# Seven products for the gate half of a projection, values split at the PSUM eviction, and four decay gates moved into the heads

## The chip, the cores and the metric

The kernel runs on one core of one Trainium2 chip. The metric is the device time of one execution in microseconds (us). The core has five engines, each with its own instruction queue in order: TensorE (PE in the profile, with PEld for its weight loads), VectorE (DVE), ScalarE (ACT), GpSimd (POOL) and SyncE (SP, which here only issues DMAs). DMAs are issued from the queues of SP, ACT and POOL.

## The reference, cut to what matters

A trunk of two layers on 512 tokens of width 1024 in float32: a gated linear attention (GLA) with 4 heads, a gated FFN, a softmax attention, a second FFN. The change lies in the GLA alone:

```python
h = rmsnorm(x, norm_mix[0])
q, k, v, g, r = split(h @ w_in)            # 512, 512, 1024, 1024, 32 columns
la = log_sigmoid(r_dir @ w_up + b_up)/16   # for each direction and head: the decay "gates"
o  = gla_chunked(q, k, v, la_f) + flip(gla_chunked(flip(q), flip(k), flip(v), flip(la_b)))
x  = x + (rmsnorm(o, norm_w) * silu(g)) @ w_out
```

In `gla_chunked`, q and k are multiplied by exp of plus and minus the sums of la within chunks of 64 tokens; masked products within a chunk and a carried state across chunks give o.

## The kernel before, in words

**Number format.** Each float32 operand of a matmul is split into a high part (rounded to fp32r) and a low part (the rest), and a product is three matmuls: high by high, high by low, low by high. For weights, `Weights` (L145 on) does this: a piece of 128x1024 is loaded by SP into one of 5 `raw` buffers (L161), ScalarE copies the high part into one of 4 `wh` buffers, and VectorE subtracts for the low part into one of 4 `wl` buffers (`split`, L240). For the sources in `by_dma`, `low_dma` (L204) does without VectorE: ScalarE writes the high part and the negative of it, and a DMA from POOL's queue, issued by `flush` (L233), adds the original onto the negative. `piece` (L253) hands a piece to the matmuls and makes `ahead` more. For FFN weights marked as sums, `summed` (L209) forms differences of quarters, so that eight block products become seven.

**The GLA** (`gla`, L487) runs in this order:

1. The vg projection, x @ [v | g], token by token rows: four segments of 512 columns (v first half, v second half, g first half, g second half). A segment (`seg`, L498) is 8 slices of x's width (k) x 4 token blocks (j) x 3 matmuls of 128x128 by 128x512 (L440), into four PSUM banks; `seg_out` (L505) has VectorE scale each bank by the token's norm and write it in float32 to `v` or `g`.
2. After segment 0: the squares of x and the token norm (`ms`, L394; `rtok`, L398), the small projection r (`rp`, L541) and its split `rst`.
3. The gates: eight (4 heads x 2 directions). `gate(n)` (L555) is one matmul (z, L559), then Abs, Exp, Ln on ScalarE, a sum, a scan and small steps on VectorE, and three Exp. `GATE_STEPS` (L30) puts all eight beside the matmuls of segments 1 to 3 (`beside`, L593).
4. The heads, from L767: the k and q projections from `w_kq` (`kproj`, `qproj`, feature by feature, L408 to L410 through `feature_steps`), `factors` and `keys` (exp factors times q and k on VectorE, `end` on POOL), `rows` (transposes of the keys and their split, L652 to L655), `inner` (L668), `masked` (L675 to L681), `values` (L684: the head's columns of v are split, 16 pairs of a ScalarE copy at L690 and a VectorE subtraction at L691 in all), `outer` (the state, L711, and the chunk's own part, L724), `outputs` (L735), `gated` (norm and silu(g), L738), `tail` (transposes, L759). The order across heads is written out by hand in the loop at L773. Silu of g (L770) comes before head 0.
5. The out projection (`out_steps`, L450) with `x += ...` at L473.

**Order.** The program is a list of instructions without engines' queues; at build time a scheduler puts each engine's instructions in order by their place in the list and by estimates of when they are ready. `issue_after` forces one behind another. On the chip each queue is then fixed. Buffers with one tag turn over: `g` has 22 of 128x1024, `x` four of 128x1024 (x itself), `u` three, `t` five and `sq` three of 128x512; PSUM has `acc` 3, `s` 2, `pt` 2 and `po` 1 banks.

Of the kernel before, what the change touches and what calls it, by code (L numbers as in the profile page):

```python
# [29 lines left out]
GATE_STEPS, GATE_LAG = (1, 3, 5, 7, 10, 12, 15, 17), 2  # L30
# [42 lines left out]
def hybrid_encoder_kernel(  # L73
# [71 lines left out]
    class Weights:  # L145
# [3 lines left out]
        def __init__(self):  # L149
            self.todo, self.made, self.by_dma, self.pending = [], {}, [], []  # L150
            self.sums, self.last, self.fine = set(), None, []
            self.loaded, self.strip = {}, {}
            self.loads, self.wide, self.turn = LOADS, 0, 0

        def add(self, src, strips=None, pieces=2):
            for i in strips or range(src.shape[0]):
                self.todo += [(src, i, h) for h in range(pieces)]
                if pieces > 2:
                    self.sums.add((id(src), i))

# [11 lines left out]
        def load(self, key):  # L172
            src, i, h = key
            if (id(src), i) in self.sums:
# [7 lines left out]
        def make(self, key):  # L182
            src, i, h = key
            self.load(key)
# [104 lines left out]
    for a in (w_vg, w_kq, w_gout):  # L289
        W.add(a)  # L290
# [5 lines left out]
    W.by_dma += [(a, 1) for a in qk_order + [w_av]] + [(w_aout, 2)]  # L296
# [190 lines left out]
    def gla(norm, nxt):  # L487
# [7 lines left out]
        v = [big(F32, "v") for _ in range(NT)]  # L495
        g = [big(F32, "g") for _ in range(NT)]
# [16 lines left out]
        for c in range(KC):  # L513
            norm.square(c)
        norm.tokens()
        seg_out(ps, v, 0)
        sync.dma_start(mfull, scan_mask)
        smask = cp.tile([P, P], U8, name="smask")
        tri = gc[:, 896 : 896 + P]
        make_lower_triangular(nc, tri, val=1.0, diag=False)  # L520
        dve.tensor_copy(smask, tri)
        cw = cp.tile([P, 2 * 2 * FC * 4], F32, name="cw")


# [12 lines left out]
        pool.tensor_tensor(gst[64:96, :], graw[64:96, :], gst[64:96, :].bitcast(F32), ALU.subtract)  # L537
        rp = bank("acc", "rp")
# [7 lines left out]
        rst = sp.tile([P, S], F32R, tag="t", bufs=5, name="rst")  # L546
# [5 lines left out]
        EK, FK = {}, {}  # L552
        act.preload_act_table_set("natural_log_exp_and_others")

        def gate(n):  # L555
# [5 lines left out]
            a = tmp("u", "ga")  # L561
            act.activation(a, z, AF.Abs, bias=b)
            m = tmp("t", "gm")
# [24 lines left out]
            act.activation(fk[:, here], fk[:, here], AF.Exp, scale=1.0 / 16)  # L588
# [8 lines left out]

        seg_out(seg(1, beside), v, 1)
        seg_out(seg(2, lambda n: beside(KC + n)), g, 0)
        seg_out(seg(3, lambda n: beside(2 * KC + n)), g, 1)  # L600

        oh = [None] * KC

        def kproj(h):
            kqt = big(F32, "kq")
            psk = bank("acc" if h else "pt", "k")
            for last in feature_steps(*W.half(w_kq, 2 * h), norm.hl, psk):
# [8 lines left out]
        def qproj(h, kqt):  # L616
            psq = bank("acc" if h else "pt", "q")
            last = feature_tile(*W.half(w_kq, 2 * h + 1), norm.hl, psq)
# [65 lines left out]
        def values(h):  # L684

            th, tl = pair("wh", NH, F32R, "vrh"), pair("wl", NL, F32R, "vrl")
            for s in range(NT):
                r = v[s][:, h * DV : (h + 1) * DV]
                hi = th[:, s * DV : (s + 1) * DV]
                act.activation(hi, r, AF.Copy)  # L690
                dve.tensor_tensor(tl[:, s * DV : (s + 1) * DV], r, hi.bitcast(F32), ALU.subtract)  # L691
            return [(th[:, s * DV : (s + 1) * DV], tl[:, s * DV : (s + 1) * DV]) for s in range(NT)]
# [76 lines left out]
        for j in range(NT):  # L769
            on_act = act.activation(g[j], g[j], AF.Silu)  # L770
        last = qproj(0, kqt)

        for h in range(GH):  # L773
            factors(h, kqt)
            if h == 0:
# [8 lines left out]
            elif h < GH - 1:  # L784
                last = outputs(h - 1, st, og, last)
                gated(h - 1, og)
                kts, last = rows(h, ends, last)
                banks, last = inner(h, last)
                at = masked(banks)
                _, kqt = whole(kproj(h + 1))  # L790
# [607 lines left out]
```

## Time and profile before

| | |
|---|---|
| median of 3 runs | 1097.81 us (1097.74 to 1098.18) |
| the profiled execution, its own time | 1096.11 us |
| its span, first to last instruction | 1094.0 us |
| granted TensorE clock | 1.0 of full speed |
| vg projection, L440 with the gates' z beside it | 6.0 to 100.5 us |
| GLA heads | 100.5 to 178.6 us |
| out projection of the GLA to the next norm | 178.6 to 232.5 us |

One execution is profiled. Its page gives the busy time of each engine, the chain of work that ended last, and groups of instructions: line, engine, operation, tile names (out<-in), shapes and count, then busy us and the mean ns of one, then the idle time of the engine before them and who ended it. A matmul's own length overlaps its neighbours', so the time that a matmul takes is read from a row of many in the chain, not from the mean of its group. In lists of waits the numbers are the total in us, the times, and the longest.

### The profile page before, as it was taken

How to read it: one execution, taken by the hardware profiler on the slowest of the kernel's cores; microseconds unless marked ns; L12 is line 12 of the kernel's file. 1: busy time of each engine (PE TensorE's matmuls, PEld its weight loads, DVE VectorE, ACT ScalarE, POOL GpSimd, SP SyncE). 2: the span in 40 equal slices, each digit the busy share in tenths (PEclk: the TensorE clock that was granted, in tenths of full speed). 3: DMA queues.
4: the chain of work that ended last, by engine and by line, in shares of the span. 5: the costliest groups of instructions: out<-in, count | busy, mean ns of one | idle time of the engine just before them, and what ended most of it. 6: DMA issues, size and time to landing. Idle time of an engine off the chain costs nothing.

```text
span 1094.0 us, 17377 instructions
## 1 busy us (share of the span) xinstructions
PE 1086.3 (99%) x6716; PEld 975.8 (89%) x6716; DVE 870.8 (80%) x1301; ACT 683.1 (62%) x1086; POOL 126.6 (12%) x138
## 2 busy tenths in 40 slices
PE   9999999999999999999999999999999999999998
PEld 7888888888899999999988888788889999999997
DVE  6686776549999899988855578765999889998892
ACT  6565344459775676657664677746977567665660
POOL 0100123022000100010014343002100010001000
PEclk9999999999999999999999999999999999999999
DMA  7323123478634733365757474557944373226542
GB/s 274 133 96 96 58 78 110 139 186 204 152 99 115 155 117 97 95 157 134 248 137 165 122 222 144 169 173 186 216 106 135 98 161 114 101 88 154 135 174 77
DMA packets 52882, 153.76 MB, mean 141 GB/s; under 512 B 6208, under 2 KB 6720, under 8 KB 52800
## 3 DMA queue, kind: packets, MB, share of 16 engines
q1 hardware_dynamic: 36192, 110.56, 31.6%
q0 software_dynamic: 11712, 33.56, 16.9%
q10 hardware_dynamic: 4896, 8.55, 2.1%
q8 instruction: 52, 0.85, 0.3%
q14 instruction: 30, 0.25, 0.1%
HBM read 110.70 MB, written 14.68 MB: 115 GB/s over the span
## 4 chain that ended last, share of the span: by engine, by line
PE 96%; DVE 2%; ACT 1%; DMA 1%; issue 0%; SPq 0%; DVEq 0%; ACTq 0%
PE r L879 37%; PE vg L440 8%; PE op L466 8%; PE up L408 6%; PE up L409 6%; PE up L410 6%; PE dn L409 2%; PE dn L410 2%; PE dn L408 2%; PE av L440 1%; PE o L735 1%; PE A L408 1%; PE A L409 1%; PE A L410 1%; PE B L410 1%; PE B L408 1%
## 5 line engine op out<-in xcount | busy, mean ns | idle before, releaser
L248 DVE TENSOR_TENSOR wl<-raw,wh 128x1024 fp32r<-128x1024 f32 x152 | 185.2, 1220 | 34.1 <-ACT wh L247 33.9
L247 ACT ACTIVATE wh<-raw 128x1024 fp32r<-128x1024 f32 x152 | 158.5, 1052 | 84.4 <-PE op L466 22.6
L879 PE MATMUL r<-gu,wh 128*128 128x256 f32 x896 | 161.8, 283 | 0.0
L879 PE MATMUL r<-xt,wh 128*128 128x256 f32 x832 | 151.2, 283 | 0.0
L879 PEld LDWEIGHTS r<-gu,wh 128*128 128x128 f32 x896 | 140.2, 192 | 0.7
L879 PEld LDWEIGHTS r<-xt,wh 128*128 128x128 f32 x832 | 130.1, 192 | 0.5 <-ACT wh L247 0.2
L879 PE MATMUL r<-gu,wl 128*128 128x256 f32 x448 | 126.6, 283 | 0.0
L879 PE MATMUL r<-xt,wl 128*128 128x256 f32 x416 | 117.4, 283 | 0.0
L879 PE MATMUL r<-nh,wh 128*128 128x256 f32 x312 | 88.9, 285 | 0.7 <-ACT r L907 0.7
L879 PE MATMUL r<-nh,wl 128*128 128x256 f32 x312 | 88.3, 283 | 0.0
L879 PE MATMUL r<-nl,wh 128*128 128x256 f32 x312 | 88.3, 283 | 0.0
L879 PEld LDWEIGHTS r<-gu,wl 128*128 128x128 f32 x448 | 85.9, 192 | 0.0
L440 PE MATMUL vg<-wh,xhl 128*128 128x512 f32 x256 | 79.9, 390 | 1.0 <-DVE wh L245 1.0
L879 PEld LDWEIGHTS r<-xt,wl 128*128 128x128 f32 x416 | 79.7, 192 | 0.0
L409 PE MATMUL up<-nl,wh 128*128 128x512 f32 x192 | 74.9, 390 | 0.0
L408 PE MATMUL up<-nh,wh 128*128 128x512 f32 x192 | 74.9, 390 | 0.0
L410 PE MATMUL up<-nh,wl 128*128 128x512 f32 x192 | 74.7, 389 | 0.0
L466 PE MATMUL op<-oT,wh 128*128 128x512 f32 x256 | 72.1, 394 | 0.0
L879 PEld LDWEIGHTS r<-nh,wh 128*128 128x128 f32 x312 | 59.8, 192 | 3.1 <-ACT r L907 2.9
L879 PEld LDWEIGHTS r<-nl,wh 128*128 128x128 f32 x312 | 59.8, 192 | 0.2
L879 PEld LDWEIGHTS r<-nh,wl 128*128 128x128 f32 x312 | 59.8, 192 | 0.0
L440 PEld LDWEIGHTS vg<-wh,xhl 128*128 128x128 f32 x256 | 47.9, 188 | 11.4 <-ACT sq L382 1.2
(263 smaller groups left out, 2676.8 us busy)
## 6 DMA issues: line engine op xcount, KB each, us to landing
raw<-in_w_up_dram SPq DMA_DIRECT2D x84, 512.0 KB, 4.5
raw<-in_w_down_dram SPq DMA_DIRECT2D x44, 512.0 KB, 3.7
wl<-raw POOLq DMA_DIRECT2D x16, 512.0 KB, 5.2
ring<-p ACTq DMA_DIRECT2D x32, 256.0 KB, 2.7
raw<-in_w_vg_dram SPq DMA_DIRECT2D x12, 512.0 KB, 4.3
wl<-in_w_up_dram POOLq DMA_DIRECT2D x12, 512.0 KB, 7.9
raw<-in_w_kq_dram SPq DMA_DIRECT2D x8, 512.0 KB, 3.6
raw<-in_w_gout_dram SPq DMA_DIRECT2D x8, 512.0 KB, 3.7
```

The costliest lines, as they stand in the source:

```text
L247: act.activation(hi[:, sl], r[:, sl], AF.Copy)
L248: dve.tensor_tensor(lo[:, sl], r[:, sl], hi[:, sl].bitcast(F32), ALU.subtract)
L408: mm(ps, wh, mh, start=start, stop=False)
L409: mm(ps, wh, ml, start=False, stop=False)
L410: return mm(ps, wl, mh, start=False, stop=stop)
L440: mm(ps[j][:, :width], hl[k][i == 2][:, j * P : (j + 1) * P], (wl if i == 1 else wh)[:, sl], start=k == 0 and i == 0, stop=k == KC - 1 and ...
L466: mm(pss[ng][n], wt[:, sl], mv, start=k == 0 and i == 0, stop=k == KC - 1 and i == 2)
L735: last = mm(og[s], l, r, start=False, stop=i == len(parts) - 1, skip_group_check=True)
L879: mm(dst, w[:, sl], m, start=start and j == 0 and a == 0, stop=j == len(pairs) - 1 and a == 2, skip_group_check=True)
```

## The change

1. **Segments 2 and 3 (g) become seven block products** (`seg_seven`). Tokens are halved (near, far), the k slices are taken in pairs (even, odd), the 1024 columns are halved. The eight block products of this 2x2 by 2x2 scheme become seven, after Strassen and Winograd, each of 4 pairs x 2 token blocks x 3 matmuls of 512 columns, in the order 1, 7, 6, 4, 5, 2, 3, accumulating in three sets of two banks that are read between products: ScalarE for 1, 7 and 6, VectorE for 4, 5, 2 (adding onto g) and 3.
2. **Their operands**: `token_sums(p)` forms the four combinations of x's quarters for pair p: ScalarE scales x[2p] and x[2p+1] by the norm weights (2 of 128x512), VectorE adds and subtracts (4 of 128x256), and `low_dma` splits the result (2 of 128x1024 on ScalarE, a 512 KB accumulating DMA). Pairs 0 and 1 stand right behind segment 0's matmuls and ahead of the r weights, the squares and the norm; pairs 2 and 3 in segment 1. `make_vg` forms the weight combinations: a VectorE subtraction of 128x1024 for product 7, two for 6, one for 3, in each of two halves, besides the split of each of the 14 half products. Pieces are made 3 ahead.
3. **v leaves PSUM as high and low parts**: ScalarE writes the high part, VectorE subtracts. The low parts take the four `x` buffers, so x is loaded again from `xT` (eight DMAs on SP) after the last head's matmuls. `values` only takes slices.
4. **Gates**: 0 and 1 in segment 1, 2 and 3 in the sixth product, 4 and 5 in head 0 (at its start and behind its `outer`), 6 and 7 in head 1. The table for Exp and Ln is loaded again after Silu.
5. **All of w_kq by `low_dma`**, pieces 2 ahead; the first k and q projections use `s` banks; `rst` sits in an `sq` buffer.

The diff, cut to its core (branches that these constants never take, the renamed arguments and the new layout of w_vg on the host are left out; the layout stores the four quarters of g's weights in place of strips 4 to 7):

```diff
-GATE_STEPS, GATE_LAG = (1, 3, 5, 7, 10, 12, 15, 17), 2
+KQ_DMA = 4
+KQ_AHEAD = 2
+LATE_GATES = {0: (4,), 30: (5,), 1: (6,), 31: (7,)}
+SEVEN_BANKS = (("pt", "pt"), ("acc", "acc"), ("acc", "s"))
+GATE_STEPS, GATE_LAG = (1, 4, 18, 19, 99, 99, 99, 99), 1
+VG_ORDER = (1, 7, 6, 4, 5, 2, 3)
+VG_AHEAD = 3
+VG_RAW = {1: (4, "g"), 7: (5, "raw"), 6: (6, "raw"), 2: (7, "raw")}
+SUMS_FIRST = 2
+SUMS_AT = {0: 2, 2: 3}
...
+        def load_vg(self, i, half):
+            if i not in VG_RAW or (i, half) in self.vg:
+                return
+            strip, tag = VG_RAW[i]
+            self.vg[i, half] = t = big(F32, "raw") if tag == "g" else pair("raw", NR, F32, "raw")
+            sync.dma_start(t, w_vg[strip, :, half * 2 * S : (half + 1) * 2 * S])
+
+        def make_vg(self, i, half):
+            self.load_vg(i, half)
+            a11, a21, a22, a12 = (self.vg.get((n, half)) for n in (1, 7, 6, 2))
+            r = {1: a11, 6: a11, 4: a22, 5: a21, 2: a12, 3: a12}.get(i)
+            if i == 7:
+                r = pair("raw", NR, F32, "sum")
+                dve.tensor_tensor(r, a21, a11, ALU.subtract)
+            elif i == 6:
+                dve.tensor_tensor(a21, a21, a22, ALU.subtract)
+                dve.tensor_tensor(a11, a11, a21, ALU.subtract)
+            elif i == 3:
+                dve.tensor_tensor(a12, a12, a11, ALU.subtract)
+            hi, lo = self.two()
...
+                self.split(hi, lo, r)
+            return hi, lo
...
-    for a in (w_vg, w_kq, w_gout):
+    W.add(w_vg, range(4))
+    W.todo += [(w_vg, -i, half) for i in VG_ORDER for half in range(2)]
+    for a in (w_kq, w_gout):
         W.add(a)
...
-    W.by_dma += [(a, 1) for a in qk_order + [w_av]] + [(w_aout, 2)]
+    W.by_dma += [(w_kq, KQ_DMA)] + [(a, 1) for a in qk_order + [w_av]] + [(w_aout, 2)]
...
-        def seg_out(ps, dst, h):
+        def seg_out(ps, h):
             for j in range(NT):
-                o = dst[j][:, h * S : (h + 1) * S]
+                if h == 0:
+                    v[j] = v[j][0], pair("x", KC // 2, F32R, "vl")
+                hi, lo = (a[:, h * S : (h + 1) * S] for a in v[j])
                 r = norm.rtok[:, j : j + 1]
-                dve.tensor_scalar(o, ps[j], r, None, ALU.mult)
+                act.activation(hi, ps[j], AF.Copy, scale=r)
+                dve.scalar_tensor_tensor(lo, ps[j], r, hi.bitcast(F32), ALU.mult, ALU.subtract)
+
+        def token_sums(p):
+            y = big(F32, "xs")
+            for i in range(2):
+                act.activation(y[:, i * S : (i + 1) * S], x[2 * p + i], AF.Copy, scale=norm.weight(2 * p + i))
+            b11, b12, b21, b22 = (y[:, n * H : (n + 1) * H] for n in range(4))
+            dve.tensor_tensor(b11, b12, b11, ALU.subtract)
+            dve.tensor_tensor(b12, b12, b22, ALU.add)
+            dve.tensor_tensor(b22, b22, b11, ALU.add)
+            dve.tensor_tensor(b21, b21, b22, ALU.subtract)
+            hi, lo = big(F32R, "xt"), big(F32R, "xt")
+            W.low_dma(hi, lo, y)
...
+        def seg_seven(between):
+            r = lambda j: norm.rtok[:, j : j + 1]
+            near, far = slice(0, S), slice(S, 2 * S)
+            first, second, third = ([bank(tag, "vg") for tag in tags] for tags in SEVEN_BANKS)
+            n = 0
+            for i, ps in zip(VG_ORDER, (first, second, first, second, first, third, first)):
+                for half in range(2):
+                    wh, wl = W.piece(w_vg, -i, half, VG_AHEAD)
+                    for o in range(2):
+                        p, sl = 2 * half + o, slice(o * S, (o + 1) * S)
+                        xh, xl = q[p][i]
+                        for j in range(2):
+                            js = slice(j * P, (j + 1) * P)
+                            for a, (m, w) in enumerate(((xh, wh), (xh, wl), (xl, wh))):
+                                mm(ps[j], m[:, js], w[:, sl], start=i in (1, 7, 2) and p == 0 and a == 0,
+                                   stop=i in (4, 2, 3) and p == 3 and a == 2, skip_group_check=True)
+                        if o == 0:
+                            W.flush()
+                    between(n)
+                    n += 1
...
         ps = seg(0)
+        for p in range(SUMS_FIRST):
+            token_sums(p)
...
-        rst = sp.tile([P, S], F32R, tag="t", bufs=5, name="rst")
+        rst = sp.tile([P, S], F32R, tag="sq", bufs=3, name="rst")
...
-        seg_out(seg(1, beside), v, 1)
-        seg_out(seg(2, lambda n: beside(KC + n)), g, 0)
-        seg_out(seg(3, lambda n: beside(2 * KC + n)), g, 1)
+        seg_out(seg(1, beside_seg), 1)
+        g = [big(F32, "g") for _ in range(NT)]
+        seg_seven(lambda n: beside(KC + n))
...
         def values(h):
...
+            return [tuple(a[:, h * DV : (h + 1) * DV] for a in v[s]) for s in range(NT)]
...
+        with tc.issue_after(turns[max(turns)].ins):
+            for j in range(NT):
+                on_act = act.activation(g[j], g[j], AF.Silu)
+        with tc.issue_after(on_act.ins):
+            turns["table"] = act.preload_act_table_set("natural_log_exp_and_others")
...
         for h in range(GH):
+            gates_for(h)
             factors(h, kqt)
...
             st, og, last, on_dve = outer(h, kts, at, vs, last)
+            gates_for(h + 30)
...
+        for p, t in enumerate(x_tiles()):
+            for i in range(2):
+                sync.dma_start(x[2 * p + i], xT[(2 * p + i) * P : (2 * p + i + 1) * P, :])
```

More of the change, by code (lines that the diff above doesn't have):

```diff
@@ L605, in kproj @@
             kqt = big(F32, "kq")
-            psk = bank("acc" if h else "pt", "k")
-            for last in feature_steps(*W.half(w_kq, 2 * h), norm.hl, psk):
+            psk = bank("acc" if h else "s", "k")
+            for last in feature_steps(*W.half(w_kq, 2 * h, KQ_AHEAD), norm.hl, psk):
+                if h == 0:
+                    beside(next(late_gates))
                 yield last, kqt
@@ L616, in qproj @@
         def qproj(h, kqt):
-            psq = bank("acc" if h else "pt", "q")
-            last = feature_tile(*W.half(w_kq, 2 * h + 1), norm.hl, psq)
+            psq = bank("acc" if h else "s", "q")
+            last = feature_tile(*W.half(w_kq, 2 * h + 1, KQ_AHEAD), norm.hl, psq)
             dve.scalar_tensor_tensor(kqt[:, :S], psq, DK ** -0.5, norm.R, ALU.mult, ALU.mult)
```

108 lines of the change are left out of this document (75 added, 33 removed).

## The prediction

> **What bounds the kernel now.** I read the busy totals first, then who TensorE waited for, then the chain that ended last, then busy time by stage.
>
> ```profile
> span 1094.0 us, 17377 instructions
> PE 1086.3 (99%) x6716; PEld 975.8 (89%) x6716; DVE 870.8 (80%) x1301; ACT 683.1 (62%) x1086; POOL 126.6 (12%) x138
> ```
> ```profile
> PE warm L324 <- DVE bd L330: 1.3, 1, 1.3
> PE vg L440 <- DVE wh L245: 1.0, 1, 1.0
> PE r L879 <- ACT r L907: 0.7, 1, 0.7
> PE o L724 <- DVE atl L681: 0.3, 2, 0.2
> ```
> ```profile
> 29.09 3.79 PE rp L541 x16
> 84.18 16.32 PE vg L440 x72
> 176.93 1.64 PE o L724 x12
> ```
>
> TensorE (PE) is busy for 1086.3 of 1094.0 us, and its waits, listed as total, times and longest, are tenths of a microsecond after the start; inside the gated-linear-attention heads only the 0.3 us at L724 is named. So the kernel lasts as long as TensorE's list of matmuls, and a change pays by shortening the list, as long as no new wait opens. The third view gives the price of one 512-column matmul in the vg projection: 72 in 16.32 us, 0.2267 us each, one behind the other. (The 389 ns that the groups show for one is its length with the overlap.)
>
> Busy time by stage, each pair of numbers being busy us and instructions:
>
> ```profile
> 6.00:28.30 22.30, 22.30 (x99) 18.09 (x99) 17.61 (x28) 14.69 (x24) 0.00 (x0) 1.00 0.83 296
> 28.30:33.30 5.00, 5.00 (x30) 4.27 (x29) 2.98 (x7) 2.38 (x3) 3.77 (x4) 1.00 0.52 183
> 33.30:56.05 22.75, 22.75 (x102) 18.80 (x101) 16.23 (x25) 12.49 (x21) 0.12 (x1) 1.00 0.34 116
> 56.05:100.50 44.45, 44.45 (x197) 36.79 (x197) 34.42 (x53) 27.14 (x44) 0.00 (x0) 1.00 0.32 107
> 100.50:122.10 21.60, 21.43 (x117) 18.37 (x116) 13.97 (x21) 9.75 (x16) 2.08 (x2) 1.00 0.17 49
> 290.00:340.00 50.00, 50.00 (x355) 47.04 (x355) 47.80 (x69) 33.14 (x51) 0.00 (x0) 1.00 0.31 96
> ```
>
> The columns are PE, weight loads, DVE (VectorE), ACT (ScalarE), POOL, granted clock, DMA. The rows are segment 0 of vg, its end, segment 1, segments 2 and 3, the first part of the heads, and a piece of the first FFN. The last one matters: there VectorE is 47.80 of 50 us busy, 95.6%, beside the same kind of work (weights added, split, and read by seven products), and TensorE loses nothing.
>
> **The change part by part. (1) The matmuls.** Segments 2 and 3 are 2 x 8 x 4 x 3 = 192 matmuls of 512 columns. The seven products are 7 x 4 pairs of rows x 2 token blocks x 3 = 168 of the same shape, each with its own 128x128 stationary operand as before. 24 fewer at 0.2267 us: **-5.44 us**. All else on TensorE stays; four of the eight gate matmuls only move into the heads. The Trainium skill ("TensorE: Matmul & The Clock Gate", section "Back-to-back issue gap") gives a sustained 131 ns for a matmul of 512 columns in a real stream; by it 24 matmuls would be worth 3.1 us. The chain above disagrees with 226.7 ns, so I go by the chain.
>
> **(2) VectorE in the projection.** Prices:
>
> ```profile
> L248 DVE TENSOR_TENSOR wl<-raw,wh 128x1024 fp32r<-128x1024 f32 x152 | 185.2, 1220 | 34.1 <-ACT wh L247 33.9
> L247 ACT ACTIVATE wh<-raw 128x1024 fp32r<-128x1024 f32 x152 | 158.5, 1052 | 84.4 <-PE op L466 22.6 <-DVE raw L228 15.3 <-PE q L409 11.1
> L227 DVE TENSOR_TENSOR sum<-raw,raw 128x1024 f32<-128x1024 f32 x42 | 51.1, 1217 | 0.0
> L583 DVE TENSOR_TENSOR ga<-ga,t 128x256 f32<-128x256 f32 x6 | 2.5, 417 | 0.0
> L564 DVE TENSOR_SCALAR gm<-z,prm 128x512 f32<-128x512 f32 x5 | 3.7, 748 | 3.3 <-ACT ga L562 3.3
> L567 DVE TENSOR_TENSOR gm<-gm,ga 128x512 f32<-128x512 f32 x5 | 3.5, 691 | 1.3 <-ACT ga L566 1.2
> L572 DVE TENSOR_TENSOR_SCAN ga<-gconst,gm 128x512 f32<-128x512 f32 x3 | 3.7, 1221 | 0.1
> L580 DVE COPY t<-ga 128x4 f32<-128x4 f32 x6 | 1.0, 168 | 0.2
> L582 DVE TENSOR_TENSOR fk<-ga,t 128x3 f32<-128x3 f32 x6 | 1.0, 159 | 0.2
> ```
>
> A gate costs VectorE 0.748 + 0.691 + 1.221 + 0.168 + 0.159 + 0.417 = 3.40 us. From 28.3 to 100.5 us VectorE was busy 2.98 + 16.23 + 34.42 = 53.6 us. Out go four gates (-13.6) and the two kq splits that fell here (-2.4; their low parts now come by DMA). In come six more splits (14 pieces for 8: +7.3), eight subtractions of weights (product 7 one, 6 two, 3 one, in two halves each: +9.8) and the token sums of pairs 2 and 3 (8 x 0.417 = +3.3). The sixteen evictions stay sixteen, of about the same length. Sum 58.0 us, or 61.3 if pairs 0 and 1 spill over from segment 0. The stretch gets shorter: 72.2 - 5.44 - four gate matmuls (0.9) = 65.9 us. So VectorE is to be **88 to 93%** busy, below the 95.6% that cost nothing. Pieces are made three ahead, with four slots: piece n+3 may be split when piece n starts and is needed 3 x 12 x 0.2267 = 8.2 us later; its longest chain (two subtractions, ScalarE's copy of about 1.05 us, the low part) is 4.7 us. I cost this at 0. If the cover goes, the price is rival B's.
>
> **(3) The start.** The sums of pairs 0 and 1 are written ahead of the squares, which the token norm waits for.
>
> ```profile
> 19.48 1.36 ACT L382 ACTIVATE sq<-x 128x512 f32<-128x512 f32 x2 [0.76 <-DVE sq L386]
> 28.14 0.95 PE L394 MATMUL ms<-ones,sq 128*128 128x1 f32 x8
> L373 ACT ACTIVATE xhl<-x,prm 128x512 fp32r<-128x512 f32 x32 | 22.8, 712 | 9.0 <-DVE x L1030 2.7 <-DMA x<-in_xT_dram 2.1 <-DVE x L473 1.9
> ```
>
> ScalarE gets 4 x 0.712 + 4 x 1.05 = 7.0 us more, and segment 0 leaves it 22.30 - 14.69 = 7.6 us. So it fits, barely. The last square ended at 20.8 us; behind all of the added work, and behind the copies of rw and gst (1.9 us, estimated from L247 by their 768 and 1024 columns), it ends at 29.7 and its sum at 30.4, against 28.1 when the norm's matmuls start. Ends: 0 and 2.3 us. Some of the squares will fill gaps while the sums wait for VectorE, so I take the nearer third, **+0.8**. The v evictions become ScalarE's high part and then VectorE's low part: about 0.7 us later for a bank that segment 1 reads at its third token block, 0.7 us after 33.3 against 32.1: nothing.
>
> **(4) Low parts of kq by DMA.**
>
> ```profile
> wl<-raw POOLq DMA_DIRECT2D x16, 512.0 KB, 5.2
> DMA to landing us min/median/max: 3.6/6.2/9.1
> ```
>
> The first piece gets its slot when the twelfth of the fourteen half products starts; its low part is read 8.2 + 0.45 us later. Two copies (2.1) and a median landing of 5.2 make 7.3; with the longest landing of all accumulating DMAs, 9.1, it is 11.2. Ends 0 and 2.6; ScalarE also has a gate there, so **+0.3**. Later pieces are two ahead at 5.4 us each: 10.9 us of cover, 0. What waits behind a late low part is all of TensorE, in order. POOL's queue takes an issue of 0.9 us each time; ahead of the keys' products that is slack, since the keys are transposed only after the next projection.
>
> **(5) The heads.**
>
> ```profile
> L691 DVE TENSOR_TENSOR vrl<-v,vrh 128x256 fp32r<-128x256 f32 x16 | 9.1, 612 | 0.0
> L690 ACT ACTIVATE vrh<-v 128x256 fp32r<-128x256 f32 x16 | 5.4, 405 | 6.2 <-PE o L724 3.7 <-PE k L409 2.5
> L565 ACT ACTIVATE ga<-ga 128x512 f32<-128x512 f32 x5 | 3.1, 627 | 0.1
> L770 ACT ACT_TABLE_LOAD x1 | 1.3, 1283 | 0.0
> ```
>
> VectorE gains four gates (13.6) and loses the splits of v (9.1) and of kq (six or so, 7.3): less work than before. ScalarE loses 5.4, gains about 8.4 of negative copies, four gates of five such activations (13.6 with the small one) and a table load of 1.3: some 18 us over heads in which it was 9.75 of 21.60 us busy. Capacity is no matter; order is. Gate 4 stands ahead of head 0's factors and holds one of three `u` buffers that the key and mask splits turn over. Gates 5 to 7 have a 5.4 us projection behind them. Ends: 0, and one scan (1.22) of delay in each gate, 4.9. The waits in these heads today add up to 0.3 us, and a VectorE split that now delays the mask (L248 ahead of L681) goes; I take **+0.5**.
>
> **(6) x is loaded again.**
>
> ```profile
> x<-in_xT_dram SPq DMA_DIRECT2D x8, 256.0 KB, 5.4
> 203.30 1.28 DVE L473 TENSOR_TENSOR x<-x,op 128x512 f32<-128x512 f32 x2 [1.91 <-PE op L466]
> ```
>
> The last values are read at 178.6 us (the chain's L724 row), and x is first needed at 203.3: 24.7 us for eight loads. The out projection hides it: 0; without that cover each microsecond of lateness at L473 is one of the end. On SP the next loads of weights stand behind the eight; the out projection's own were issued before them.
>
> Sum: -5.44 + 0.8 + 0.3 + 0.5 = **-3.8 us**. The profiled execution took 1096.11 us around its span of 1094.0; the same execution would be 1092.3 with a span of 1090.2. It lies 1.7 us under the median of 1097.81; from that median the forecast is **1094.0**.
>
> **The rivals.** A, *clean*: none of the three waits comes. Then -5.44, with the 0.3 us in the heads -5.8: 1092.0. For it speak 99% and 95.6%; against it the 0.6 us that segment 0 leaves ScalarE.
>
> B, *slower: VectorE becomes the bound of the seven products*. The subtractions, copies and low parts of one piece are a chain over two queues in order, so VectorE may not reach 88%. In segments 2 and 3 it ran at 34.42 of 44.45, 77%, though with nothing to hurry it. At 77% its 58.0 us last 74.9, 9.0 over the 65.9: -5.44 + 9.0 + 1.6 = +5.2, 1103.0. It eats the gain below 81% (58.0/71.3) and is slower by 0.2% below 79%. The FFN's 95.6% speaks against it. To see: TensorE waiting at the products for wl.
>
> C, *given back*: the start, the first kq piece and the heads near their upper ends, 2.3 + 2.6 + half of 4.9 = 7.3 at the most; at two thirds 4.9: 1097.3.
>
> D, *the change doesn't do what it says*: the products free less time than their count. The sixteen matmuls of L541, also into one bank with a new stationary operand each, came 0.237 us apart (3.79/16). At that spacing the 168 take 39.8 us instead of 38.1, the gain is 3.7, and with the waits -2.1: 1095.7. The 0.2267 of the 72 in a row speaks against it.
>
> **How the numbers follow.** Forecast 0.58, A 0.14, B 0.13, C 0.13, D 0.02. About 0.2%, 2.2 us, is what a measurement of this kernel can tell from no change: faster is below 1095.6, slower above 1100.0. Forecast and A are faster: 0.72. C and D are within it: 0.15. B is slower: 0.13. The range goes from A's 1092.0 to 1098.6, which takes in D and most of C; left out are B and C's tail up to 1099.7.
>
> **What would show it.** Right: the new group of vg matmuls counts 168, half a product lasts 2.7 us, TensorE's waits stay under 2 us in sum between 28 and 180 us, and VectorE is near 90% from 28 to 94. Wrong at (1): the spacing isn't 0.227. At (2): waits for wl or wh within the products. At (3): TensorE waits for a square or for the norm near 28 us. At (4): the first key projection waits for a DMA. At (5): waits at L668, L711 or L724. At (6): L473 waits for a DMA.

## The result, and the profile after

The changed kernel takes 1101.48 us (median of 9 runs, 1099.16 to 1102.17) against 1097.70 us (median of 9, 1095.67 to 1098.18) for the kernel before: a ratio of 1.0037, 95% interval 1.0026 to 1.0047. It is 3.8 us slower, where 3.8 us faster was forecast. Its profiled execution, the longest of the nine, took 1102.17 us around a span of 1100.5 us, against 1094.0 before.

The page's totals of the changed kernel:

```profile
span 1100.5 us, 17420 instructions
...
PE 1087.3 (99%) x6692; PEld 975.4 (89%) x6692; DVE 877.9 (80%) x1307; ACT 713.0 (65%) x1116; POOL 135.7 (12%) x150
```

TensorE has the 24 matmuls less (6716 became 6692), and yet is as busy as before, 1087.3 us. So some matmuls have become slower, besides the waits. The waits of TensorE, as total, times and longest:

```profile
PE kv L455 <- DVE kq L730: 2.3, 1, 2.3
PE ms L441 <- DVE sq L433: 1.9, 1, 1.9
PE warm L371 <- DVE bd L377: 1.3, 1, 1.3
PE vg L487 <- DVE wh L290: 1.2, 1, 1.2
PE vg L595 <- DVE wl L293: 0.8, 2, 0.5
...
PE o L839 <- ACT ath L801: 0.6, 1, 0.6
```

New are kv (the products that form the state), ms (the sums of the squares for the norm), the two at the products (L595) and ath (the high part of the masked products). Three marks on TensorE's timeline tell where the time went: the end of segment 0 (the first instruction behind it), the first matmul of head 0's key projection, and the sums of the second norm. Before, the first was at 28.14 (quoted in the prediction); the other two:

```profile
100.34 0.39 PE L408 MATMUL k<-xhl,wh 128*128 128x512 f32 x1
...
232.34 0.95 PE L394 MATMUL ms<-ones,sq 128*128 128x1 f32 x8
```

After, in the same order:

```profile
30.25 3.79 PE L645 MATMUL rp<-xhl,rw 128*128 128x512 f32 x16
...
101.16 0.39 PE L455 MATMUL k<-xhl,wh 128*128 128x512 f32 x1
...
238.76 0.95 PE L441 MATMUL ms<-ones,sq 128*128 128x1 f32 x8
```

| stretch | before | after | difference |
|---|---|---|---|
| to the end of segment 0 | 28.14 | 30.25 | +2.1 |
| from there to the key projection | 72.20 | 70.91 | -1.3 |
| heads and out projection, to the second norm | 132.00 | 137.60 | +5.6 |
| the rest | 861.66 | 861.74 | +0.1 |

The first difference is none of the change's. In this execution the first 16 or so matmuls of segment 0 ran at half pace, and the whole of segment 0 took some 2 us longer; e1 and e2 below have the same code up to there and run it at full pace. It is seen in 9 of this study's 14 profiles. The runs of one kernel, too, lie in two groups some 1.7 us apart (the kernel before near 1096.0 and near 1097.7), which may have the same cause, so a median of a few runs can be off by that much. Without these 2.1 us the profiled pair differs by 4.4 us, near the medians' 3.8.

The second stretch should have shrunk by 5.44 us for 24 matmuls and 0.9 for four gate matmuls that moved behind it. It shrank by 1.3, so 5.0 us were lost. The third holds those 0.9 us now, so 4.7 us were lost there. Busy time by stage (columns as in the prediction; the last three are granted clock, DMA share, GB/s):

```profile
30.25:61.20 30.95, 29.04 (x127) 23.70 (x126) 24.48 (x36) 20.86 (x31) 5.16 (x5) 0.94 0.33 95
61.20:101.16 39.96, 39.15 (x171) 31.76 (x170) 32.92 (x40) 27.53 (x37) 2.58 (x3) 1.00 0.53 145
30.25:101.16 70.91, 68.19 (x297) 55.46 (x296) 57.41 (x75) 48.40 (x67) 7.75 (x8) 0.98 0.44 123
101.16:123.00 21.84, 21.58 (x114) 18.30 (x112) 12.78 (x23) 20.79 (x30) 5.45 (x6) 1.00 0.82 193
```

In the products (second row) VectorE is busy 32.92 of 39.96 us, 82%, and TensorE waits 0.8 us for it: it is not the bound. The granted clock is 0.94 in segment 1, where it was 1.00.

**The loss at the norm.** ScalarE, VectorE, GpSimd and TensorE around the norm's sums, each from its timeline (start, duration, instruction, and in brackets the idle time before it):

```profile
30.45 1.06 ACT L292 ACTIVATE wh<-raw 128x1024 fp32r<-128x1024 f32 x1 [2.21 <-PE vg L487]
31.42 1.14 ACT L429 ACTIVATE sq<-x 128x512 f32<-128x512 f32 x2
32.46 1.04 ACT L628 ACTIVATE gst<-graw 128x1024 fp32r<-128x1024 f32 x1
33.41 0.63 ACT L429 ACTIVATE sq<-x 128x512 f32<-128x512 f32 x1
```
```profile
32.68 4.25 DVE L433 TENSOR_TENSOR sq<-sq,sq 128x512 f32<-128x512 f32 x3
```
```profile
33.64 2.75 POOL L629 TENSOR_TENSOR gst<-graw,gst 32x1024 fp32r<-32x1024 f32 x1 [7.46 <-issue]
```
```profile
37.08 1.02 PE L441 MATMUL ms<-ones,sq 128*128 128x1 f32 x8 [1.91 <-DVE sq L433]
```

The last three squares stand in ScalarE's queue behind a weight copy that can't start until segment 0 gives its buffer back (30.45, after 2.21 us of idling), and the last one also behind gst's copy. Before, the last square ended at 20.8 us. Then three additions take 4.25 us where 3 x 0.69 are due. The chain of waits shows the long one:

```profile
34.27 2.68 DVE sq L433
```

It lies beside GpSimd's subtraction of 2.75 us and ends 0.6 us after it, at 36.95. TensorE waits 1.91 us. At 0.69 us the addition would have ended at 34.96, before the 35.17 at which TensorE began to wait: so it takes both, a square so late that its addition meets the subtraction, and the subtraction. And then the clock falls. Stage rows of one microsecond each:

```profile
37.00:38.00 1.00, 0.92 (x9) 0.95 (x9) 1.00 (x1) 0.00 (x0) 0.00 (x0) 1.00 0.01 4
38.00:39.00 1.00, 1.00 (x4) 0.81 (x5) 0.23 (x2) 0.00 (x0) 0.55 (x1) 0.54 0.00 0
39.00:40.00 1.00, 1.00 (x4) 0.81 (x3) 0.17 (x1) 0.27 (x1) 0.93 (x3) 0.50 1.00 262
40.00:41.00 1.00, 1.00 (x3) 0.72 (x3) 0.55 (x1) 1.00 (x3) 0.02 (x1) 0.50 0.62 229
41.00:42.00 1.00, 1.00 (x7) 0.79 (x6) 0.86 (x2) 1.00 (x2) 0.00 (x0) 0.76 0.08 33
```

For about 3.5 us TensorE is granted half its clock: 0.46 + 0.50 + 0.50 + 0.24 = 1.7 us of its work are lost, and the profile counts them as busy. So this one wait costs 1.9 + 1.7 = 3.6 us in this execution.

**The loss in head 1.** The chain, from the timelines of VectorE, ScalarE and GpSimd:

```profile
137.68 1.21 DVE L680 TENSOR_TENSOR_SCAN ga<-gconst,gm 128x512 f32<-128x512 f32 x1
...
142.16 0.17 DVE L387 TENSOR_SCALAR ors<-oss 128x4 f32<-128x4 f32 x1 [2.07 <-ACT junk L858]
143.49 1.66 DVE L864 SCALAR_TENSOR_TENSOR g<-o,ors,g 128x256 f32<-128x256 f32 x4 [1.16 <-POOL ors L389]
145.07 0.68 DVE L730 TENSOR_TENSOR kq<-k,R 128x512 f32<-128x512 f32 x1
```
```profile
139.80 0.20 ACT L696 ACTIVATE fk<-fk 128x3 f32<-128x3 f32 x1 [2.00 <-DVE fk L690]
139.91 0.37 ACT L858 ACTIVATE junk<-o 128x256 f32<-128x256 f32 x1
...
141.66 0.38 ACT L858 ACTIVATE junk<-o 128x256 f32<-128x256 f32 x1
```

Gate 6 stands at this head's start. Its small Exp (L696) waits 2.00 us on ScalarE for VectorE, where the scan and the gate's last steps stand. Behind it stand the squares of head 0's outputs (junk), behind these the root ors, behind ors the gated products (L864) on VectorE, and behind these, in order, the eviction of head 2's key (L730). That eviction frees the bank into which the kv products write, and TensorE waits 2.3 us for it. The slow clock follows here too, from 147 to 151 us, and takes another 1.7 us.

The mean granted clock of the nine runs is 0.998 in six, 0.997 in two (the profiled one is one of them) and 0.995 in one. An estimate: two such stretches, 3.4 of 1100 us, make 0.997, and one makes 0.998. So most of the nine had only one of the two, and the profiled execution shows more of this loss than the median has.

### The profile page after: what moved, and what is told of

It is laid out like the page before. It is cut to its first block, busy times and chain, and to the rows that moved or that the text cites. A ratio compares the mean times of both kernels' runs of the same rounds, so it can differ in the third digit from the quotient of the medians.

```text
span 1100.5 us, 17420 instructions
## 1 busy us (share of the span) xinstructions
PE 1087.3 (99%) x6692; PEld 975.4 (89%) x6692; DVE 877.9 (80%) x1307; ACT 713.0 (65%) x1116; POOL 135.7 (12%) x150
## 4 chain that ended last, share of the span: by engine, by line
PE 86%; DVE 5%; ACT 5%; issue 2%; DMA 1%; SPq 0%; POOL 0%; DVEq 0%; ACTq 0%
PE r L1008 37%; PE op L513 8%; PE up L455 6%; PE up L456 6%; PE up L457 6%; PE dn L456 2%; PE dn L455 2%; PE dn L457 2%; PE vg L595 1%; PE av L487 1%; DVE wl L293 1%; PE A L455 1%; ACT wh L292 1%; PE A L457 1%; PE A L456 1%
## 5 line engine op out<-in xcount | busy, mean ns | idle before, releaser
L293 DVE TENSOR_TENSOR wl<-raw,wh 128x1024 fp32r<-128x1024 f32 x148 | 180.2, 1219 | 30.4 <-ACT wh L292 28.4
L292 ACT ACTIVATE wh<-raw 128x1024 fp32r<-128x1024 f32 x148 | 154.1, 1052 | 71.7 <-PE op L513 22.7
L250 ACT ACTIVATE wh<-raw 128x1024 fp32r<-128x1024 f32 x36 | 38.0, 1055 | 35.8 <-PE up L456 11.5
L293 DVE TENSOR_TENSOR wl<-sum,wh 128x1024 fp32r<-128x1024 f32 x44 | 53.6, 1219 | 5.0 <-ACT wh L292 5.0
```

Of the source, the lines that this page charges most:

```text
L292: act.activation(hi[:, sl], r[:, sl], AF.Copy)
L293: dve.tensor_tensor(lo[:, sl], r[:, sl], hi[:, sl].bitcast(F32), ALU.subtract)
```

## The experiments

Two losses, then: one at the norm and one in head 1, each a wait followed by slow matmuls. The rivals were that the products give less than their count, and that any repair only moves the wait. In the diffs, lines with "-" are the changed kernel's, and "..." stands for lines left out. One more part of the change matters here, which the core of the diff above does not show: the copies of rw and gst on ScalarE, and gst's subtraction on GpSimd, stand ahead of the squares in the changed kernel. Before, they stood behind the norm.

**e1: token sums behind the squares.**

```diff
         ps = seg(0)
-        for p in range(SUMS_FIRST):
-            token_sums(p)
...
         for c in range(KC):
             norm.square(c)
+        for p in range(SUMS_FIRST):
+            token_sums(p)
         norm.tokens()
```

> The token sums of pairs 0 and 1 stand behind the squares instead of ahead of them; nothing else differs. Theory (a queue's order at the norm): in the changed kernel TensorE waited 1.9 us for the last sum of squares at 37 us and then ran at a granted clock of 0.5 for 3.4 us; with the squares first that wait and the slow stretch go, some 3 us, so about 1098.5, and the norm's matmuls start before 34 us. New risk within the theory: the v evictions now stand behind two token sums on ScalarE (6.4 us), which can give back 1 to 2 us at segment 1's third token block. Rival (VectorE cannot keep up with the products): the place of the sums does not matter, within 1 us of 1101.5, and the waits for wl in the products grow.

Measured: 1106.58 us (1104.44 to 1106.99), ratio 1.0093 [1.0076, 1.0110]. The wait at ms is gone, but one of 1.9 us stands at bc, the matmuls that spread the token norms rtok over the partitions; the v evictions come late behind the sums and the products wait 1.4 us for vl (a low part of v) and 1.3 for wl (a low part of weights); the clock falls three times and takes 5.1 us. On VectorE and GpSimd ahead of bc:

```profile
32.11 2.54 DVE L569 TENSOR_TENSOR xs<-xs 128x256 f32<-128x256 f32 x1
```
```profile
31.61 2.77 POOL L627 TENSOR_TENSOR gst<-graw,gst 32x1024 fp32r<-32x1024 f32 x1 [30.23 <-ACT gst L626]
```

This time GpSimd's subtraction stretches a token sum, 2.54 us for 0.42, and the step from ms to rtok stands behind it on VectorE. Moving the whole of the sums behind the squares only moves the loss, and adds to it.

**e2: the gst subtraction on VectorE.**

```diff
-        pool.tensor_tensor(gst[64:96, :], graw[64:96, :], gst[64:96, :].bitcast(F32), ALU.subtract)
+        dve.tensor_tensor(gst[64:96, :], graw[64:96, :], gst[64:96, :].bitcast(F32), ALU.subtract)
```

> The 32x1024 subtraction for gst moves from GpSimd to VectorE. Theory (two engines hold each other up): one sum of squares lasted 2.68 us in the changed kernel beside GpSimd's 2.75 us subtraction, against 0.69 us elsewhere; with the subtraction on VectorE (an estimate of 1.2 us for it) all sums last 0.7, the norm's matmuls start about 1 us earlier and the wait shrinks from 1.9 us to about 1; some 1 to 2 us less, about 1100. Rival (the sum was late for ScalarE's square): its length stays over 2 us and the time is the same within 0.5 us or longer by the added 1.2.

Measured: 1101.72 us (1101.24 to 1103.27), ratio 1.0050 [1.0035, 1.0065].

```profile
33.42 0.69 DVE L433 TENSOR_TENSOR sq<-sq,sq 128x512 f32<-128x512 f32 x1
```

Each of these additions takes 0.69 us now. So the stretch does come from GpSimd's subtraction beside them. The wait at ms falls to 1.1 and one of 0.9 follows at bc, and neither brings the slow clock. But nothing is gained: a token sum's DMA is now late for product 7 (a wait of 2.8 us, with the slow clock behind it). Neither this move nor e1's, at one place each, repairs the start.

**e3: gated products behind the key projection.**

```diff
-GATED = 0
+GATED = 2
```

> The gated outputs of the head before are written behind the next key projection, not ahead of the transposes. Theory (order on VectorE in head 1): the 2.3 us wait of the state's matmuls for the key eviction, which stood behind the gated products on VectorE, which waited for the power on GpSimd and for squares on ScalarE behind gate 6, goes, and with it 1.7 us of a slow clock: about 1097.5. Rival (the gates' own work in the heads is too much): the wait only moves, to the mask (L839 waits for atl or ath) or to the transposed outputs (L874), and the time stays above 1100.

Measured: 1104.32 us (1102.98 to 1104.79), ratio 1.0069 [1.0054, 1.0084]. The wait at kv is gone; the outputs at L839 now wait for the gated products to free their banks, 3.8 us in two waits. The rival was right: it only moves.

**e4: all gates in the products.**

```diff
-LATE_GATES = {0: (4,), 30: (5,), 1: (6,), 31: (7,)}
+LATE_GATES = {}
...
-GATE_STEPS, GATE_LAG = (1, 4, 18, 19, 99, 99, 99, 99), 1
+GATE_STEPS, GATE_LAG = (1, 4, 18, 19, 20, 21, 22, 24), 1
...
```

A line not shown lets Silu follow the last gate's last large Exp in place of its small one.

> Gates 4 to 7 are worked at the end of the products and in the first key projection, none in the heads; Silu waits for the last of them. Theory (late gates cost the heads): the waits in heads 0 and 1 (0.6 us for ath, 2.3 for the key eviction, and slow clocks behind them) go; some 4 to 5 us less, if ScalarE and VectorE, with four gates of 3.4 us each more between 85 and 110 us, do not make the key projection wait; so between 1096.5 and 1100. Rival (the wait in head 1 comes from the place of the gated outputs, not from the gates): the wait at the state's matmuls stays, and the time stays near 1101.

Measured: 1108.83 us (1105.44 to 1109.22), ratio 1.0105 [1.0089, 1.0122]. The waits in head 1 go, but the gates pile up at the end of the projection: head 0's first products wait 7.7 us for VectorE, and the slow clock takes 6.8 us in all. So the late gates are cheaper than gates crowded into the last products and the first key projection. The kernel before worked all eight beside segments 1 to 3 without a wait, so this speaks of e4's places, not of early gates as such.

**e5: gate 6 beside gate 7, behind head 1's outer products.**

```diff
-LATE_GATES = {0: (4,), 30: (5,), 1: (6,), 31: (7,)}
+LATE_GATES = {0: (4,), 30: (5,), 31: (6, 7)}
```

> The sixth late gate (h=3, d=0) is worked with the seventh behind head 1's outer products instead of ahead of head 1's factors. If the hold-up of head 1 (the gate's scan, then the squares of the outputs, the gated products and, behind them on VectorE, the eviction of head 2's key) is what costs the heads their time, the wait of 2.3 us at the kv products and the 1.7 us of slow clock behind it go: 101.5 - 4.0 + up to 1.5 for a queue that is now fuller ahead of head 2's queries, so 1097.5 to 1099. If two gates back to back only move the wait, TensorE waits 2 to 4 us at head 2's first products (rows, inner) and the time stays at 1101 to 1103.

Measured: 1103.22 us (1102.37 to 1104.33), ratio 1.0058 [1.0043, 1.0073]. The rival was right again. The wait at kv is gone, and head 2's rows wait for the tail of head 0, whose eviction stands behind two gates on VectorE:

```profile
PE kt L773 <- DVE oT L879: 3.0, 1, 3.0
PE ms L441 <- DVE sq L433: 1.9, 1, 1.9
```

**e6: the start in another order.** Only ScalarE's scalings of x stay in segment 0, behind the squares; the copies of rw and gst go back to where they were before the change, and the sums' subtractions and splits come behind the norm.

```diff
         ps = seg(0)
-        for p in range(SUMS_FIRST):
-            token_sums(p)
-        rraw = sp.tile([P, KC * 32], F32, tag="sq", bufs=3, name="rraw")
...
         for c in range(KC):
             norm.square(c)
         norm.tokens()
+        ys = [scaled(p) for p in range(SUMS_FIRST)]
         seg_out(ps, 0)
...
+        rraw = sp.tile([P, KC * 32], F32, tag="sq", bufs=3, name="rraw")
...
+        for p, y in enumerate(ys):
+            token_sums(p, y)
```

> Of the token sums of pairs 0 and 1 only ScalarE's four scalings stay in segment 0, behind the squares; the subtractions and the xt copies, and the copies of rw and gst, come after the norm, where before.py has rw and gst. If the start lost its time to this order, the wait at ms (1.9 us) and the half clock behind it (1.7 us) go: about 1098 (1097.5 to 1099). If the added work only moves, as with all of it behind the squares, the waits come back at bc, at vl or at the weights of segment 1, and the time stays at 1101 to 1106.

Measured: 1095.50 us (1094.35 to 1097.10, 10 runs) against 1096.89, ratio 0.9989 [0.9980, 0.9999]. No wait is left between segment 0 and the heads; behind segment 0 one large one remains in the whole profile:

```profile
PE kv L455 <- DVE kq L733: 1.9, 1, 1.9
```

The first instruction behind segment 0 and the first matmul of the key projection:

```profile
30.05 0.95 PE L441 MATMUL ms<-ones,sq 128*128 128x1 f32 x8
...
95.86 0.39 PE L455 MATMUL k<-xhl,wh 128*128 128x512 f32 x1
```

The stretch between them is 65.81 us. It is 5.1 us shorter than the 70.91 of the changed kernel. So the order at the start cost all of the 5.0 us lost there, the 0.8 at the products included, and the time fell by more than expected. The first theory holds for the start, and with it repaired the kernel is as fast as the one before, or a little faster. The edit moves two things behind the norm at once, the sums' subtractions and splits and the copies of rw and gst. e1 and e8, which leave rw and gst ahead of the squares, each have a wait at bc; but no run moves only one of the two, so how they share the loss is open.

**e7: e6 with e5's gates.**

```diff
-LATE_GATES = {0: (4,), 30: (5,), 1: (6,), 31: (7,)}
+LATE_GATES = {0: (4,), 30: (5,), 31: (6, 7)}
```

> The two edits before together. If start and heads are the two whole losses and independent, their gains add: about 1094 (1093.5 to 1096), with no wait of over 1 us between 28 and 180 us and the gain of 24 matmuls visible: faster than the kernel before by 0.2 to 0.3%. If one of the two still leaves its wait, 1097 to 1099.

Measured: 1097.91 us (1094.57 to 1098.71), ratio 1.0006 [0.9996, 1.0015]. Not 1094: the wait of 3.0 us at head 2's rows is there as in e5. The start's gain stays, the head's loss sits elsewhere.

**e8: the change without its seven products.** Segments 2 and 3 as before, no token sums; all else of the change stays.

```diff
-        seg_seven(lambda n: beside(KC + n))
+        for i in range(2):
+            ps = seg(2 + i, lambda n: beside((1 + i) * KC + n))
+            for j in range(NT):
+                dve.tensor_scalar(g[j][:, i * S : (i + 1) * S], ps[j], norm.rtok[:, j : j + 1], None, ALU.mult)
```

> The change without its seven products: segments 2 and 3 as before (192 matmuls), no token sums; v as high and low parts, kq by DMA, rw and gst ahead of the squares, the four late gates and the reload of x stay. If the products are worth 5.44 us and lose some 1.5 us to waits within them, and the token sums make the start's loss: 1101.5 + 5.4 - 1.0 - 3.5 = about 1102.4, of which head 1's wait and slow clock of 4 us remain in full. If instead the products gain nothing (matmuls spaced wider, or lost again by VectorE), it is at or below 1098: the start's 3.5 go and nothing is added.

Measured: 1104.00 us (1102.85 to 1105.32), ratio 1.0069 [1.0052, 1.0086]. Slower than with the products, as the first theory had it: they earn something. It had a part wrong. I had put the start's loss down to the token sums; with these left out, bc still waits 1.7 us, with the slow clock behind it: with gst ahead of the squares, the root for rtok stands behind gst's subtraction in GpSimd's queue. That is some 0.9 us of it: the root's operand is ready at 33.2 us, and the root starts at 34.15.

**e9 and e10: e6, with gate 6 in head 0.** In e9 only the gate's first half (up to its scan) is worked behind head 0's outer products, in e10 the whole gate. There no tail stands behind it. e9 (-6 works the first half) and e10, beside e6's edit:

```diff
-LATE_GATES = {0: (4,), 30: (5,), 1: (6,), 31: (7,)}
+LATE_GATES = {0: (4,), 30: (5, -6), 1: (6,), 31: (7,)}
...
-                for _ in gates[n]:
-                    pass
+                for _ in gates[abs(n)]:
+                    if n < 0:
+                        break
```
```diff
-LATE_GATES = {0: (4,), 30: (5,), 1: (6,), 31: (7,)}
+LATE_GATES = {0: (4,), 30: (5, 6), 31: (7,)}
```

> The start as in e6, and of gate 6 (h=3, d=0) the first half (its matmul, three activations, two VectorE operations) is worked behind head 0's outer products with gate 5; only its scan and factors stay ahead of head 1's. There is no tail in head 0, so nothing of the kind that waited in e5 and e7 stands there. If head 1's loss is the eviction of head 2's key held up behind the gated products, and that chain starts 2 us earlier, the wait at the kv products of 1.9 us falls under 0.5 us, the slow clock behind it (1.7 us) does not come, and the time is e6's less 3 to 3.6: 1092 (1091.5 to 1093). If the wait moves to head 1's rows or its products of keys and queries, 1094.5 to 1097.

> As e9, but the whole of gate 6 behind head 0's outer products. VectorE has 1.95 us more there ahead of the low parts that head 1 needs. If the theory of e9 holds and there is room for a whole second gate, the same time as e9 within 1 us; if not, a wait of 1 to 3 us at head 1's first rows, with slow clock behind it where it is near 2 us: 1094 to 1097.

Measured: e9 1094.64 us (1093.02 to 1095.18), ratio 0.9970 [0.9958, 0.9982]; e10 1092.45 us (1092.02 to 1094.11) against 1097.54, ratio 0.9958 [0.9942, 0.9973]. e9 misses its 1092: the wait at kv is gone, but one of 1.3 us stands in head 1 for atl, the low part of the masked products; e10 has none over 0.6 from segment 1 to the end of the heads, and no microsecond of slow clock. e10's three marks and its stage:

```profile
28.28 0.95 PE L441 MATMUL ms<-ones,sq 128*128 128x1 f32 x8
...
94.09 0.39 PE L455 MATMUL k<-xhl,wh 128*128 128x512 f32 x1
...
228.79 0.95 PE L441 MATMUL ms<-ones,sq 128*128 128x1 f32 x8
```
```profile
28.28:94.09 65.81, 65.81 (x297) 54.55 (x296) 52.97 (x72) 50.24 (x68) 10.12 (x10) 1.00 0.57 150
```

From segment 0 to the key projection it is 65.81 us, TensorE without a gap, at full clock: 6.39 less than the 72.20 before, where 24 matmuls and four gate matmuls are 6.34. e6, e7 and e9 have the same 65.81 there. In head 1 the eviction of the key no longer stands behind the gated products, but waits for its own matmuls:

```profile
131.15 1.66 DVE L867 SCALAR_TENSOR_TENSOR g<-o,ors,g 128x256 f32<-128x256 f32 x4 [1.16 <-POOL ors L389]
...
135.21 0.69 DVE L733 TENSOR_TENSOR kq<-k,R 128x512 f32<-128x512 f32 x1 [0.83 <-PE k L457]
```

Heads and out projection last 134.70 us, 2.9 less than in the changed kernel and 2.7 more than before; 0.9 of these are the gate matmuls and some 0.9 small waits (ath 0.6, ek 0.3, atl 0.3, against 0.3 before). The other 0.9 I did not find.

**e11: e10 without the seven products**, e8's edit on e10 (lines with "-" are e10's here):

```diff
-        ys = [scaled(p) for p in range(SUMS_FIRST)]
...
-        seg_seven(lambda n: beside(KC + n))
+        for i in range(2):
+            ps = seg(2 + i, lambda n: beside((1 + i) * KC + n))
...
```

> e10 without its seven products: segments 2 and 3 as before with 192 matmuls and no token sums, everything else as e10. As e10 has no waits of note from segment 1 to the end of the heads, this is the price of the products by themselves. If 24 matmuls are worth 24 x 0.2267: e10 + 5.4 = 1097.9 (1097 to 1098.8), the same as before. If a part of e10's gain came from elsewhere (the late gates, v's parts, the reload of x), it stays below 1096.

Measured: 1099.88 us (1098.79 to 1100.57), ratio 1.0029 [1.0018, 1.0041]: 0.71% above e10's ratio, about 7.8 us, and more than the 5.4 expected. The profile shows a reason:

```profile
PE z L661 <- DVE rst L649: 1.7, 1, 1.7
```
```profile
35.68 2.33 DVE L624 CAST smask<-gconst 128x128 uint8<-128x128 f32 x1
```

```profile
35.54 2.38 POOL L638 TENSOR_TENSOR gst<-graw,gst 32x1024 fp32r<-32x1024 f32 x1 [2.26 <-issue]
```

Without the sums the order around the norm is another. The cast of smask, 0.22 us in the kernel before, falls beside GpSimd's subtraction and takes 2.33; the gate's operand comes late behind it, and the first gate matmul waits 1.7 us. By the traces, the stretch from segment 0 to the key projection is 73.20 us here (29.52 to 102.72), 7.4 more than e10's 65.81. Without the wait that is 5.7 us for the products, and 5.4 by their count: their gain is real.

**e12: the changed kernel with e10's place of gate 6 alone.**

```diff
-LATE_GATES = {0: (4,), 30: (5,), 1: (6,), 31: (7,)}
+LATE_GATES = {0: (4,), 30: (5, 6), 31: (7,)}
```

> The changed kernel with gate 6 behind head 0's outer products as in e10, and its start left as it is. If head 1's hold-up and its slow clock are a loss by themselves, the wait at the kv products goes and the time falls by 3.6 to 4.0 from 1101.5: 1097.5 to 1098, with the wait of 1.9 us at ms and the slow clock behind it still there. If start and heads hang together (a late start that shifts the heads), it stays over 1099.

Measured: 1099.43 us (1097.15 to 1100.58), ratio 1.0022 [1.0011, 1.0033]. The wait at kv is gone, and key projection to second norm is 134.87 us (101.64 to 236.51), 2.7 less than the changed kernel's and the same as e10's. So the head's loss goes without a repair of the start. The median, though, lies where I had put the other case, over 1099: the same wait of 1.9 us at ms is here followed by seven microseconds of slow clock instead of 3.5, and takes 3.4 us instead of 1.7. The four runs with a mean granted clock of 0.996 or 0.997 took 1099.43 to 1100.58 us, the three with 0.998 took 1097.15 to 1098.55, near the 1097.5 to 1098 expected. That the clock makes this difference is likely, not shown.

## Why the prediction was wrong

**What held.** Step (1): 24 matmuls at 0.2267 us, -5.44; e10 shows it to 0.1 us. Rival D's spacing of 0.237 falls with it. Step (2): I gave VectorE 58.0 us of work from segment 0 to the heads, and it had 57.41, the stretched addition included, in 70.91 us; the products wait 0.8 us for it, and nothing in e10. Rival B, VectorE as the bound, falls. But the 88 to 93% of the forecast were never put to the test: VectorE was busy for 81% of this stretch in the changed kernel, and for 80% in e10 (52.97 of 65.81), where TensorE has no gap. Steps (4) and (6): no wait for a low part of kq, none for x.

**Step (3), the start, failed**: put at +0.8 with an upper end of 2.3, it cost 3.6 in the profile, and 5.1 with the waits that followed from it, as e6 shows. I added up ScalarE's durations and saw that they fit into segment 0, by 0.6 us. But they don't run when there is room: they run in the queue's order, and in it the last squares stand behind a weight copy that waits for segment 0's end. The last square ended 3.8 us behind segment 0 (34.04 and 30.25), where the estimate had 1.6 (29.7 and 28.1). Then came the stretched addition, which I did not price. The Trainium skill has the rule for it: "SBUF — State Buffer", section "Who interferes with whom", says that a VectorE instruction with two inputs in SBUF contends with a GpSimd instruction that reads SBUF, as the two share a read interface. The runs agree: 0.69 us became 2.68 beside the subtraction, and stayed 0.69 in e2, which has no GpSimd work there.

**Step (5), the heads, failed**: put at +0.5 between ends of 0 and 4.9, it cost 4.7: most of it 2.3 at kv, 1.7 of slow clock behind it and 0.6 at ath. I had seen gate 4 as the danger, and wrote that gates 5 to 7 have a projection of 5.4 us behind them. Gate 6 has none: it stands ahead of head 1's factors, and what it held up was the squares of the outputs, four steps before the eviction that TensorE needed. ScalarE, for which I said that "capacity is no matter", was busy 20.79 of 21.84 us in head 0 and had TensorE wait 0.6 us there.

**Both failed by one more thing**: I priced a wait at its length. Here a wait of about 2 us costs nearly twice that where the clock is halved behind it, and in e12 nearly three times. Rival C named the two places, but its own end was 1099.7 and the time is beyond it: with the slow clock left out, its bounds were too low. The forecast of -3.8 was about right for a kernel that does the same work in e10's order: -3.5 us in its profiled span, -0.42% in its runs. In part that is luck: e10 loses nothing at the start and for kq, where the forecast had 0.8 and 0.3, and 1.8 in the heads, where it had 0.5.

## What to carry to other kernels

When TensorE is the bound, a change of this kind is decided by where its side work stands in the in-order queues, not by whether there is room for it: for each added instruction, look for what stands ahead of it and waits, and follow what stands behind it to the next bank that TensorE needs. In this kernel, price a wait on a busy TensorE at its length and, from some 1.6 us on, at another 1.7 us for the clock, which came in most cases. Then repair waits in pairs and look again, since a single move mostly shifts the loss (e1 to e5), and only the right place (e6 and e10) keeps it gone.

## What the runs showed of the hardware

- **A short wait is mostly followed by half the clock.** Of 18 waits of 1.6 us and more that TensorE had between the norm and the end of the heads, 16 were followed by about 3.5 us at a granted clock of 0.50 (once seven, and once eleven behind 7.7 us); waits of 1.7 and 1.8 us (e11, e8) were not, nor were single waits of 1.5 us and less (in e1, two of 1.4 and 1.3 us close together were). Each stretch took 1.70 to 1.71 us, the seven microseconds of e12 3.41 and the eleven of e4 5.12: once, twice and three times the same. It does not always come: e6 and e7 have one long wait each in their profiles, and of their 20 runs 17 have a mean granted clock of 0.998 and three of 1.0, the shortest run of each among them. The Trainium skill ("TensorE: Matmul & The Clock Gate", section "What's actually happening") has the half rate come after an idle window of about 3.4 us. Here 1.9 us were enough; the length of the slow stretch is near its 3.4.
- **GpSimd's subtraction holds VectorE up**: 0.69 us became 2.68 (an addition), 0.42 became 2.54 (a token sum), each begun beside a GpSimd subtraction of 2.75 us or so. They ended 0.6 and 0.3 us behind it, about their own length, as if they had waited for its end. e11's cast, with one input, went from 0.22 to 2.33 us beside one of 2.38. The subtraction itself took 2.75 us in e8 too, with little on VectorE beside it, so nothing shows that VectorE held it up. That it is a shared port was not tested by itself; that the subtraction is the cause, e2 shows for the additions.
- **The first matmuls run at half pace in some executions of a kernel**, some 2 us on the span. It was not tested what decides it; kernels with the same code up to there are on both sides (the changed kernel, e1 and e2).
